# Splitting each tile's load over two DMA queues and moving the stores to GpSimd, in a GELU-and-multiply kernel

## The chip, the cores and the metric

The kernel runs on one core of one Trainium2 chip. The metric is the device time of one execution in microseconds; the kernel before takes 469.43 us, the median of 3 runs (469.3 to 469.44). A core has several engines with an instruction stream each. Here ScalarE (ACT in the profile) computes the GELU, VectorE (DVE) the product, and SyncE (SP), ACT and GpSimd (POOL) can issue DMA transfers. All transfers of the core, whoever issues them, are carried by 16 DMA engines; each issuing engine has a queue of its own to them.

## The reference

```python
def setup_inputs():
    batch, seq, dim = (32, 512, 2048)
    return {'x': np.random.randn(batch, seq, dim).astype(np.float32)}

def reference(x: np.ndarray) -> np.ndarray:
    half_dim = x.shape[-1] // 2
    x1, x2 = (x[..., :half_dim].copy(), x[..., half_dim:].copy())
    gelu_x1 = 0.5 * x1 * (1 + erf(x1 / np.sqrt(2)))
    return (gelu_x1 * x2).astype(np.float32)
```

The input has 16384 rows of 2048 float32 (134.2 MB), the output 16384 rows of 1024 (67.1 MB). Each output element is the GELU of an element of the left half of its row times the element at the same place in the right half.

## The kernel before

The rows are cut into 16 tiles of 1024 rows. In a tile each of the 128 partitions holds R = 8 consecutive rows (lines 26 to 28), so one partition's share of a tile is one contiguous run in memory: 64 KB of input, 32 KB of output. There are two input buffers (`x_bufs`) and two output buffers (`o_bufs`); tile i uses number i % 2 of each (lines 30 and 31).

The kernel is written with semaphores by hand. `counted` adds an increment to an instruction and keeps the running total in `n`; a wait on `n[...]` is thus a wait for everything issued so far that counts on that semaphore. A DMA adds 16 when it is complete, a compute instruction 1. `load` (line 48) is always issued on SP. `store` (line 53) takes the queue to issue on; it waits there until `mul_done` has reached its running total.

Ahead of the loop (lines 63 to 73) ACT issues a transfer of 4 KB into a scrap tile, the "opening"; SP issues the lower half (rows 0 to 3 of every partition) and the upper half (rows 4 to 7) of tile 0, with a semaphore each (`first`), and the whole of tile 1.

The loop at line 75 then goes over the tiles. A tile is computed in steps: rows 0 to 4 and 5 to 7 for an ordinary tile; rows 0-1, 2-3 and 4-7 for the first and the last. For each step ACT computes the GELU from the left half of `x_bufs[k]` into `o_bufs[k]` (line 87), and DVE multiplies it in place by the right half (line 95). Before the first step of a tile, ACT waits for `ready[k]` (line 85). Both the load of tile i and the store of tile i - 2 count on this one semaphore, so the wait covers the new input and the free output buffer.

After the steps the tile is stored: tiles 1 to 13 whole, on ACT's queue (line 112); tile 0 in two halves, also on ACT (line 107); tile 14 whole and tile 15 in two halves on SP (lines 105 and 110). When tile i is multiplied, SP issues the load of tile i + 2 into the same buffer (lines 113 to 115). A store on ACT waits for the multiply in ACT's instruction stream, and the GELU of the next tile stands behind it.

At the end ACT waits for the opening transfer, the semaphores are cleared, and SP waits until the last stores have landed (line 125).

Of the kernel before, what the change touches and what calls it, by code (L numbers as in the profile page):

```python
# [1 line left out]

# [4 lines left out]

GELU = mybir.ActivationFunctionType.Gelu


@with_exitstack
def kernel(
    ctx: ExitStack,
    tc: tile.TileContext,
    x: bass.AP,
    out: bass.AP,
):
    nc = tc.nc
    P = nc.NUM_PARTITIONS

    x_flat = x.flatten_outer_dims()
    out_flat = out.flatten_outer_dims()
    n_rows, dim = x_flat.shape
    half = dim // 2

    R = 8
    x_t = x_flat.rearrange("(n p r) d -> n p r d", p=P, r=R)
    o_t = out_flat.rearrange("(n p r) d -> n p r d", p=P, r=R)
    n_tiles = x_t.shape[0]
    x_bufs = [nc.alloc_sbuf_tensor(f"x{k}_tile", [P, R, dim], x.dtype) for k in range(2)]  # L30
    o_bufs = [nc.alloc_sbuf_tensor(f"o{k}_tile", [P, R, half], out.dtype) for k in range(2)]

    first = [nc.alloc_semaphore(f"first{j}") for j in range(2)]
    ready = [nc.alloc_semaphore(f"ready{k}") for k in range(2)]
    gelu_done = nc.alloc_semaphore("gelu_done")
    mul_done = nc.alloc_semaphore("mul_done")
    tail_stored = nc.alloc_semaphore("tail_stored")
    opened = nc.alloc_semaphore("opened")  # L40
    scrap = nc.alloc_sbuf_tensor("scrap_tile", [8, 128], x.dtype)
    n = {sem.name: 0 for sem in [*first, *ready, gelu_done, mul_done, tail_stored, opened]}

    def counted(ins, sem, by):
        ins.then_inc(sem, by)
        n[sem.name] += by

    def load(i, rows, sem):
        ins = nc.sync.dma_start(out=x_bufs[i % 2][:, rows, :], in_=x_t[i][:, rows, :])  # L49
        counted(ins, sem, 16)  # L50
        return ins

    def store(queue, i, rows, sem):
        queue.wait_ge(mul_done, n[mul_done.name])
        counted(
            queue.dma_start(out=o_t[i][:, rows, :], in_=o_bufs[i % 2][:, rows, :]), sem, 16
        )

    opening = nc.scalar.dma_start(out=scrap[:, :], in_=x_t[0][:8, 0, :128])
    counted(opening, opened, 16)
    for ins in (
        opening,
        load(0, slice(0, 4), first[0]),
        load(0, slice(4, 8), first[1]),
        load(1, slice(0, 8), ready[1]),
    ):  # L70
        tc.no_tile_sem_insts.add(ins.ins.name)
    tc.close()
    tc.compile()  # L73

    for i in range(n_tiles):
        k = i % 2
        last = i == n_tiles - 1
        pieces = i == 0 or last
        steps = ((0, 2), (2, 4), (4, 8)) if pieces else ((0, 5), (5, 8))
        for lo, hi in steps:  # L80
            rows = slice(lo, hi)
            if i == 0 and lo % 4 == 0:
                nc.scalar.wait_ge(first[lo // 4], 16)
            elif lo == 0:
                nc.scalar.wait_ge(ready[k], n[ready[k].name])
            counted(
                nc.scalar.activation(  # L87
                    out=o_bufs[k][:, rows, :], in_=x_bufs[k][:, rows, :half], func=GELU
                ),
                gelu_done,  # L90
                1,
            )
            nc.vector.wait_ge(gelu_done, n[gelu_done.name])
            counted(
                nc.vector.tensor_mul(  # L95
                    out=o_bufs[k][:, rows, :],
                    in0=o_bufs[k][:, rows, :],
                    in1=x_bufs[k][:, rows, half:],
                ),
                mul_done,  # L100
                1,
            )
            if pieces and hi % 4 == 0:
                if last:
                    store(nc.sync, i, slice(hi - 4, hi), tail_stored)
                else:
                    store(nc.scalar, i, slice(hi - 4, hi), ready[k])
        if not pieces:
            if i == n_tiles - 2:
                store(nc.sync, i, slice(0, R), tail_stored)  # L110
            else:
                store(nc.scalar, i, slice(0, R), ready[k])
        if i + 2 < n_tiles:
            nc.sync.wait_ge(mul_done, n[mul_done.name])
            load(i + 2, slice(0, R), ready[k])


    nc.scalar.wait_ge(opened, 16)
    nc.scalar.drain()  # L119
    for sem in (*first, *ready, opened):  # L120
        nc.scalar.sem_clear(sem)
    nc.vector.drain()
    nc.vector.sem_clear(gelu_done)
    nc.sync.sem_clear(mul_done)
    nc.sync.wait_ge(tail_stored, n[tail_stored.name]).then_inc(
        tail_stored, -n[tail_stored.name]
    )


# [1 line left out]
_INS = ['x']  # L131
_OUTS = [((32, 512, 1024), 'float32')]


# [23 lines left out]
```

## Time and profile before

| | |
|---|---|
| time, median of 3 runs | 469.43 us |
| profiled execution: span | 467.8 us (467.84 in the trace) |
| memory read and written | 134.22 MB and 67.11 MB, 430 GB/s over the span |
| ACT, GELU of 5 rows and 3 rows of a tile together | 7.12 us |
| DVE, product of the same | 8.76 us |
| load of a tile, from issue to landing, median | 44.4 us |
| store of a tile from ACT, from issue to landing, median | 44.7 us |
| first GELU starts | 12.79 us |
| last multiply starts | 455.76 us |

The span goes from the first to the last event of the program in one profiled execution; the time of a run has a little more around it. The profile names an engine, a line of the kernel and the operands of each group of instructions, and what ended the idle time before it. Issuing a transfer is not counted as work of its engine: such instructions appear as SPq or ACTq, with the duration of the issue alone. The records of the DMA queues count packets: a packet is one contiguous run of one partition, or a 4-byte write that adds to a semaphore. The DMA share is the mean busy share of the 16 engines; in a short stretch it can read above 1, since a packet is counted where it lands.

### The profile page before, as it was taken

The page shows a single profiled execution, that of the slowest core. Times are in us where ns is not written, and L with a number is a line of the kernel's source. Part 1 is how long each engine was busy: PE and PEld are TensorE (multiplying, and loading weights), DVE is VectorE, ACT ScalarE, POOL GpSimd, SP SyncE. Part 2 cuts the span into 40 slices and gives each one's busy share as a digit, 9 for nine tenths or more (in the row PEclk, how much of TensorE's full clock was granted, in tenths as well). Part 3 has the DMA queues.
Part 4 walks back from the last instruction along what each step waited for, and adds up shares of the span by engine and source line. Part 5 has one row for each costly group of instructions (what it writes and reads, how often), then busy time and mean ns, then how long its engine had stood idle before and what let it go on. Part 6 is the DMA issues. An engine that isn't in the chain of part 4 may idle for free.

```text
span 467.8 us, 154 instructions
## 1 busy us (share of the span) xinstructions
DVE 140.5 (30%) x34; ACT 115.5 (25%) x35; POOL 0.2 (0%) x4
## 2 busy tenths in 40 slices
DVE  0330515207051060511606115060150702507043
ACT  1320606041060410604105050050501506014060
POOL 0000000000000000000000000000000000000000
DMA  8999999999999999999999999999999999999988
GB/s 359 448 448 448 398 406 496 403 403 448 459 437 403 440 412 493 403 403 448 487 409 403 445 406 493 403 403 448 493 403 403 448 426 471 403 426 426 493 384 379
DMA packets 5057, 201.34 MB, mean 430 GB/s; under 512 B 568, under 2 KB 576, under 8 KB 576
## 3 DMA queue, kind: packets, MB, share of 16 engines
q1 hardware_dynamic: 2880, 142.61, 70.6%
q10 hardware_dynamic: 2176, 58.73, 29.1%
q14 instruction: 1, 0.01, 0.0%
HBM read 134.22 MB, written 67.11 MB: 430 GB/s over the span
## 4 chain that ended last, share of the span: by engine, by line
DMA 76%; DVE 14%; ACT 8%; ACTq 0%; SPq 0%; issue 0%
DMA out_dram<-o_tile 66%; DVE o_tile L95 14%; DMA x_tile<-in_x_dram 10%; ACT o_tile L87 8%; ACTq L119 0%; SPq L49 0%
## 5 line engine op out<-in xcount | busy, mean ns | idle before, releaser
L95 DVE TENSOR_TENSOR o_tile<-o_tile,x_tile 128x5120 f32<-128x5120 f32 (+3 forms) x34 | 140.5, 4171 | 319.7 <-ACT o_tile L87 319.7
L87 ACT ACTIVATE o_tile<-x_tile 128x5120 f32<-128x5120 f32 (+3 forms) x34 | 114.3, 3407 | 337.3 <-DMA out_dram<-o_tile 301.8
L87 ACT ACT_TABLE_LOAD x1 | 1.3, 1283 | 2.9 <-PEq L73 2.9
L142 POOL MEMSET const-bfloat16-1.0<- 128x1 bf16 x1 | 0.1, 102 | 0.0
L142 POOL MEMSET const-uint8-127<- 128x1 uint8 x1 | 0.1, 101 | 0.0
L142 POOL MEMSET const-float32-0.0<- 128x1 f32 x1 | 0.1, 99 | 0.2 <-issue 0.2
L142 POOL MEMSET const-float32-1.0<- 128x1 f32 x1 | 0.1, 98 | 0.0
## 6 DMA issues: line engine op xcount, KB each, us to landing
out_dram<-o_tile ACTq DMA_DIRECT2D x13, 4096.0 KB, 44.7
x_tile<-in_x_dram SPq DMA_DIRECT2D x2, 4096.0 KB, 16.7
out_dram<-o_tile ACTq DMA_DIRECT2D x2, 2048.0 KB, 34.4
out_dram<-o_tile SPq DMA_DIRECT2D x1, 4096.0 KB, 25.2
out_dram<-o_tile SPq DMA_DIRECT2D x2, 2048.0 KB, 7.8
x_tile<-in_x_dram SPq DMA_DIRECT2D x15, 44.4
scrap_tile<-in_x_dram ACTq DMA_DIRECT2D x1, 4.0 KB
```

The costliest lines, as they stand in the source:

```text
L87: nc.scalar.activation(out=o_bufs[k][:, rows, :], in_=x_bufs[k][:, rows, :half], func=GELU),
L95: nc.vector.tensor_mul(out=o_bufs[k][:, rows, :], in0=o_bufs[k][:, rows, :], in1=x_bufs[k][:, rows, half:],),
L142: nc = _bacc.Bacc("TRN2", target_bir_lowering=False, num_devices=1)
```

## The change

A tile's load becomes two transfers: rows 0 to 3 of each partition on SP's queue and rows 4 to 7 on ACT's, 32 KB per partition each. Tile 0 still comes wholly on SP. Tile 1's upper half is issued by ACT once tile 0's lower half has landed. For later tiles ACT waits for the multiply of tile i and then issues the upper half of tile i + 2. The stores of tiles 0 to 13 are issued by GpSimd, which has nothing else to do; the last two tiles are stored from SP as before. Since loads and stores are now on different queues, the stores get semaphores of their own (`stored`), and ACT waits for `ready[k]` and then `stored[k]` before a tile. The opening transfer and its wait at the end are gone. The computation, its steps and the two buffers of each kind stay.

```diff
-    opened = nc.alloc_semaphore("opened")
-    scrap = nc.alloc_sbuf_tensor("scrap_tile", [8, 128], x.dtype)
-    n = {sem.name: 0 for sem in [*first, *ready, gelu_done, mul_done, tail_stored, opened]}
+    stored = [nc.alloc_semaphore(f"stored{k}") for k in range(2)]
+    n = {sem.name: 0 for sem in [*first, *ready, *stored, gelu_done, mul_done, tail_stored]}
...
-    def load(i, rows, sem):
-        ins = nc.sync.dma_start(out=x_bufs[i % 2][:, rows, :], in_=x_t[i][:, rows, :])
+    def load(queue, i, rows, sem):
+        ins = queue.dma_start(out=x_bufs[i % 2][:, rows, :], in_=x_t[i][:, rows, :])
...
-    opening = nc.scalar.dma_start(out=scrap[:, :], in_=x_t[0][:8, 0, :128])
-    counted(opening, opened, 16)
+    lower, upper = slice(0, 4), slice(4, 8)
     for ins in (
-        opening,
-        load(0, slice(0, 4), first[0]),
-        load(0, slice(4, 8), first[1]),
-        load(1, slice(0, 8), ready[1]),
+        load(nc.sync, 0, lower, first[0]),
+        load(nc.sync, 0, upper, first[1]),
+        load(nc.sync, 1, lower, ready[1]),
     ):
...
             if i == 0 and lo % 4 == 0:
                 nc.scalar.wait_ge(first[lo // 4], 16)
+                if lo == 0:
+                    load(nc.scalar, 1, upper, ready[1])
             elif lo == 0:
                 nc.scalar.wait_ge(ready[k], n[ready[k].name])
+                if n[stored[k].name]:
+                    nc.scalar.wait_ge(stored[k], n[stored[k].name])
...
-                    store(nc.scalar, i, slice(hi - 4, hi), ready[k])
+                    store(nc.gpsimd, i, slice(hi - 4, hi), stored[k])
...
-                store(nc.scalar, i, slice(0, R), ready[k])
+                store(nc.gpsimd, i, slice(0, R), stored[k])
         if i + 2 < n_tiles:
             nc.sync.wait_ge(mul_done, n[mul_done.name])
-            load(i + 2, slice(0, R), ready[k])
+            load(nc.sync, i + 2, lower, ready[k])
+            nc.scalar.wait_ge(mul_done, n[mul_done.name])
+            load(nc.scalar, i + 2, upper, ready[k])
...
-    nc.scalar.wait_ge(opened, 16)
     nc.scalar.drain()
-    for sem in (*first, *ready, opened):
+    for sem in (*first, *ready, *stored):
         nc.scalar.sem_clear(sem)
```

## The prediction

> **What bounds the kernel now.** I read the page's share of each DMA queue first, then a stretch of the steady state by queue, then the same stretch by engine, and last the chain of waits around the first and the last tiles.
>
> ```profile
> span 467.8 us, 154 instructions
> DVE 140.5 (30%) x34; ACT 115.5 (25%) x35; POOL 0.2 (0%) x4
> q1 hardware_dynamic: 2880, 142.61, 70.6%
> q10 hardware_dynamic: 2176, 58.73, 29.1%
> ```
>
> q1 is SP's queue, q10 ACT's: 70.6% + 29.1% = 99.7% of the time of all 16 DMA engines lies inside packets, while the two compute engines stand idle for 70% and more. The DMA queues from 118 to 350 us, eight tiles in 232 us, and then the engines of one tile pair:
>
> ```profile
> DMA packets 2304, 100.66 MB, mean 434 GB/s; under 512 B 256, under 2 KB 256, under 8 KB 256
> q1 hardware_dynamic: 1152, 67.11, 66.7%
> q10 hardware_dynamic: 1152, 33.55, 33.5%
> ```
> ```profile
> 118.00:176.00 58.00, 17.52 (x4) 14.24 (x4) 0.00 (x0) 1.00 1.00 434
> ```
>
> Here the DMA share is 1.00. Of the 1152 packets on each queue 128 are the 4-byte semaphore writes; the other 1024 are one row group of one partition each, 64 KB for a load and 32 KB for a store. A load packet takes 0.667 x 232 x 16 / 1024 = 2.418 us, a store packet 0.335 x 232 x 16 / 1024 = 1.214 us. The sum of 100.2% says that neighbouring packets overlap a little. The packet records of the trace give it exactly: durations 2418 and 1213 ns, but from start to start on one engine 2414 and 1209 ns, and this whether the next packet is from the same queue or the other. So a byte costs the same for loads and stores, a switch between two queues costs nothing, and no engine pauses from 2.2 us (first load packet) to 467.4-467.8 us (last semaphore writes). Tile 1 in the timeline, and tile 3 in the chain of waits (start, duration, what):
>
> ```profile
> 47.02 7.12 ACT L87 ACTIVATE o_tile<-x_tile 128x5120 f32<-128x5120 f32 x2 [20.93 <-DMA x_tile<-in_x_dram]
> 51.52 8.76 DVE L95 TENSOR_TENSOR o_tile<-o_tile,x_tile 128x5120 f32<-128x5120 f32 x2 [20.97 <-ACT o_tile L87]
> ```
> ```profile
> 100.40 4.48 ACT o_tile L87
> 104.88 0.02 issue
> 104.91 8.77 DVE o_tile L95 x2
> 113.68 0.02 issue
> 113.70 44.67 DMA out_dram<-o_tile
> ```
>
> A tile that has landed is computed in 113.68 - 100.40 = 13.3 us and then spends 44.7 us in the queues. One tile's store and the next load to the same buffer, 12.58 MB, keep the engines busy for 29.0 us (58.0 us a pair, 434 GB/s). At 100.38 us they still hold a whole such batch for the other buffer, and the next is issued 13.3 us later. **The time is the sum of the packets; the waits in the chain are waits for a queue that never runs dry.** A change matters if it alters that sum, lets the queues run dry, or alters the two ends.
>
> **The change, part by part.** *Split loads.* Tiles 1 to 15 were loaded in 64-KB packets, 8 per engine and tile (128 partitions over 16 engines): 120 packets per engine become 240 of 32 KB. From start to start 2 x 1209.3 - 2414.1 = 4.5 ns more for each of the 120: +0.54 us. If durations count without the overlap, 2 x 1213 - 2418 = 8 ns: +0.96. I take 0.54, since start to start is what a full engine repeats.
>
> *Semaphore writes.* Loads go from 17 to 32 issues, each with one 4-byte packet of 9 ns on every engine: 15 x 9 = 0.135 us, less the opening transfer's one: +0.13.
>
> *The opening transfer* (8 packets of 512 B at 25 ns, on ACT's queue at 2.15 us) goes. The first load packets start at 2.20 us and take 1.64 to 2.06 us, mean 1.81, instead of 1.21. If that came from the opening transfer beside them, 0.6 us would be won; if it is the start of the reads themselves, nothing. A 25-ns packet can hardly cost 600: I take 0, bounds -0.6 and 0.
>
> *Issues.* SP's load issues (0.33 us each) stay 17: two halves of tile 0, one half each of the 15 others. ACT's 15 store issues (0.36) become 15 load issues; GpSimd gets 15 stores. ACT waits for the same multiply before its load as it did before its store, and what is queued behind it, the next tile's GELU, needs its tile landed anyhow: in the chain ACT waits there for 21.9 us. The new wait for the store of two tiles ago was inside the old wait (one semaphore counted both). On SP nothing stands behind a load but the next one and the last three stores; on POOL (busy 0.2 us) nothing stands behind a store but the next, 29 us later. All issue time lies under queues with a backlog.
>
> *GpSimd's issue latency.* No row has a store from GpSimd. From SP the way from issue to first packet is 2.20 - 0.73 = 1.5 us. A steady store is issued behind the previous tile's traffic, which lasts 29.0 - 13.3 = 15.7 us more; a longer way costs nothing until it reaches about 13 us. I take 0.
>
> *GpSimd's packets.* Not shown either. From below: if the eight rows that an engine has of a store go as one packet, 7 seams of 4.5 ns vanish in each of 15 stores: -0.5 us. From above: if every store's first packet on every engine started cold like the first packets of the run (+0.43 to +0.85 us), 15 stores give +6 to +13 us. The nearest row is ACT's store packets, the same rows between the same loads, 1209 ns from start to start: I take 0 and keep -0.5 and +13.
>
> *Order at the start.* Tile 0's upper half now shares with the upper half of tile 1, issued on ACT at 12.8 us when tile 0's lower half has landed, and from about 21 us with the first store. Worked through by turns of 32 KB: tile 0's upper half lands near 33 us (22.4 before), its multiply ends near 41 (30.6), tile 1's lower half lands near 51.5 (47.0), its upper half well ahead. Work issued by then ends at 2.8 + 38.7 (16.78 MB) + 29.0 = 70.5 us, so 19 us are queued, against 13.3 + 1.5 = 14.8 needed until the next batch moves. Nothing runs dry; about 4 us of cover are left, where before it was far more. The lead of the upper halves (some 11 us) then stays, and later tiles keep about 7 us.
>
> *The end.* When tile 15 lands (448.5 us), the store of tile 14 (4.19 MB, 9.7 us) is left. It stands behind tile 15's lower half in SP's queue, as before behind the whole tile. The first half of tile 15's store moves 455.1 - 448.5 + 1.5 = 8.1 us later, the second 460.2 - 448.5 + 1.5 = 13.2 against 9.7 + 4.8 = 14.5: covered by 1.3 us, and the last store lands as now.
>
> Sum: 0.54 + 0.13 = +0.67 us. The profiled execution: 467.84 + 0.67 = 468.5 span. The median of the runs lies 469.43 - 467.84 = 1.6 us above that span, so **470.1 us**, +0.14%. About 0.2% (0.94 us) is what a measurement can tell from no change; by that this is none.
>
> **The rivals.** *(B) GpSimd's packets are dearer: slower.* Place: the 120 store packets per engine on the third queue. Every nanosecond there adds 0.12 us; it decides from 2.3 ns, where 0.67 + 0.27 passes 0.94. For it: no GpSimd store is in the trace, and with DMA share 1.00 nothing can hide even a small cost on one engine, as tiles wait for all 16. Against: two queues alternate without any cost now. A cold start of 0.43 us per store gives 470.1 + 6.5 = 476.6; 20 ns a packet, 472.5. The Trainium skill (DMA: Bandwidth & Descriptors, "Latency and other measured facts") holds engines 7 and 15 to be usually slower with software-generated descriptors, which is how GpSimd issues, and gives no size; in this trace, which has none, all 16 engines end within 0.45 us of each other.
>
> *(C) The stores starve and the queues run dry: much slower.* If the engines take turns by packet and GpSimd's packets are far smaller than 32 KB (say 4 KB), two load queues take nearly all turns. Both buffers then fill with landed tiles, and only the older store, 9.7 us, is left while the next tile is computed and its batch started: 14.8 us. That leaves some 5.1 us idle per pair of tiles, 7 pairs: +36 us, about 507 with the extra seams (7 x 4.5 ns x 112 = 3.5 us). For it: taking turns by packet is seen, since a 64-KB load and a 32-KB store issued together land within 0.3 us (44.4 and 44.7 us). Against: every queue's packets here are as long as the contiguous run. The Trainium skill (same page, "SWDGE vs HWDGE vs iDMA") states 4096 B as the preferred packet; this trace's packets of 64 KB on the hardware queues disagree, and no run shows GpSimd's.
>
> *(D) Not slower.* The slow first packets were the opening transfer's doing and go with it: 470.1 - 0.6 = 469.5; with seams saved on the stores, 469.0. Both are still no change. For faster by 0.2% (468.5) no row offers enough: the engines are full from 2.2 us to the end.
>
> **How the numbers follow.** Forecast 0.46, own range 469.7 to 470.7 (the 8-ns seam reaches 470.5); B 0.36, mostly below 476; C 0.07; D 0.11. Range 469.0 to 476.0: it leaves out C and the far end of B, some 0.13, and a little of D. Faster 0.05 (from D). Same: 0.37 of the forecast and 0.06 of D, 0.43. Slower: 0.09 of the forecast (dearer seams), B and C, 0.52. The single likeliest case is no change, though all slower cases together weigh more.
>
> **What would show it.** Right: DMA share 1.00 and 433 to 434 GB/s in the steady stretch, three queues near 33% each, 32-KB packets of 1213 ns on all, the pair period up by 0.07 us. The store's time to landing may fall and the load halves differ by some 11 us without meaning. B shows as more time per packet on GpSimd's queue, or as one or two engines ending late; C as stretches of DMA share below 1.00 and small packets; D as first packets near 1.2 us. The forecast is wrong if DMA share drops below 1.00 anywhere between 3 and 467 us.

## The result and the profile after

| | before | changed |
|---|---|---|
| time, median of 8 runs | 469.29 us (469.19 to 469.53) | 470.52 us (470.45 to 470.73) |
| ratio | | 1.0027 (95% interval 1.0018 to 1.0035) |
| span of the profiled execution | 467.84 us | 469.2 us (469.16 in the trace) |

The changed kernel is 1.23 us slower. That is a small but real loss: the runs of the two kernels do not overlap. The first lines and the DMA queues of the changed kernel's page (packets, MB, share of 16 engines over the span):

```profile
span 469.2 us, 183 instructions
...
q1 hardware_dynamic: 2880, 79.69, 39.6%
q10 hardware_dynamic: 2160, 62.92, 31.1%
q0 software_dynamic: 2160, 58.72, 29.0%
```

q0 is GpSimd's queue. The three shares add up to 99.7%, exactly as the two did before: the engines are as full as they were, and the span is longer because they have more to do. The same queues in the steady window from 118 to 350 us, and the chain of waits (start, duration, what):

```profile
q0 software_dynamic: 1152, 33.55, 33.5%
q1 hardware_dynamic: 1152, 33.55, 33.5%
q10 hardware_dynamic: 1151, 33.52, 33.5%
```
```profile
116.92 44.77 DMA x_tile<-in_x_dram
...
175.00 44.77 DMA x_tile<-in_x_dram
...
233.09 44.76 DMA x_tile<-in_x_dram
...
349.27 44.76 DMA x_tile<-in_x_dram
```

All three queues carry 1024 packets of 32 KB (one fewer on q10 in this window) and 128 semaphore writes in the same time: 0.335 x 232 x 16 / 1024 = 1.214 us a packet, GpSimd's like the others. In the packet records, packets on one engine mostly follow each other from start to start in 1209 ns, whichever two queues they come from.

A seam is what two 32-KB packets take more than one of 64 KB. Four pairs of tiles take 349.27 - 116.92 = 232.35 us, where they took 345.70 - 113.70 = 232.00; the chain of before has:

```profile
113.70 44.67 DMA out_dram<-o_tile
...
345.70 44.73 DMA out_dram<-o_tile
```

That is 0.09 us more for a pair (0.0875), as 16 seams of 4.5 ns and 2 semaphore writes of 9 ns make it. The 15 split tiles are 7.5 pairs: 0.66 us over the run.

The rest is lost once, around the first store. The queues from 20 to 32 us, before and then changed:

```profile
q1 hardware_dynamic: 96, 4.72, 93.3%
q10 hardware_dynamic: 48, 0.79, 15.3%
```
```profile
q10 hardware_dynamic: 69, 2.26, 45.0%
q1 hardware_dynamic: 73, 1.87, 42.7%
q0 software_dynamic: 43, 0.70, 13.7%
```

From this view one can work out by how much packets are stretched, that is, how much longer they take than in the steady state. The view counts a packet, with its whole duration, in the window in which it starts. 100% is 12 us x 16 engines = 192 us. From a queue's share of that goes what its packets take in the steady state, and the remainder over 16 is the loss per engine. Before, q1 has 64 packets of 64 KB, 16 of 32 KB and 16 semaphore writes: 179.1 - 174.3 = 4.8, so 0.30 us per engine. Changed, q1 has 57 of 32 KB (1.87 MB): 82.0 - 69.3 = 12.7, 0.79 us; q10 has 69: 86.4 - 83.7 = 2.7, 0.17 us; q0's are on time. Together 0.96 us, 0.66 more than before. With the 0.66 above that is 1.32, and the spans differ by 469.16 - 467.84 = 1.32.

### The profile page after: what moved, and what is told of

Same layout as the page of the kernel before. It is cut to its first block, busy times and chain, and to the rows that moved or that the text cites. A ratio compares the mean times of both kernels' runs of the same rounds, so it can differ in the third digit from the quotient of the medians.

```text
span 469.2 us, 183 instructions
## 1 busy us (share of the span) xinstructions
DVE 140.5 (30%) x34; ACT 115.5 (25%) x35; POOL 8.3 (2%) x19
## 4 chain that ended last, share of the span: by engine, by line
DMA 76%; DVE 14%; ACT 8%; ACTq 0%; issue 0%
DMA x_tile<-in_x_dram 76%; DVE o_tile L92 14%; ACT o_tile L84 8%; ACTq L117 0%
## 5 line engine op out<-in xcount | busy, mean ns | idle before, releaser
L55 POOL DMA_DIRECT2D out_dram<-o_tile x15 | 8.1, 542 | 399.6 <-DVE o_tile L92 399.6
```

## The experiments

All times are against the kernel before, run beside them on the same chip (469.25 to 469.28 us). "Stretch" is the loss per engine computed as above. In the code cuts "..." marks lines left out.

**Stores on GpSimd alone** (the kernel before, loads whole on SP).

```diff
...
-                    store(nc.scalar, i, slice(hi - 4, hi), ready[k])
+                    store(nc.gpsimd, i, slice(hi - 4, hi), stored[k])
...
-                store(nc.scalar, i, slice(0, R), ready[k])
+                store(nc.gpsimd, i, slice(0, R), stored[k])
...
```

> The kernel before, with only the stores of tiles 0 to 13 moved to GpSimd and their own semaphores; loads whole on SP in 64-KB packets. Theory 'GpSimd's queue is only dear when it starts': steady packets 1213 ns as on ACT, but load packets stretched by 0.6 to 1.0 us per engine around the first store: +0.3 to +0.7 us against before. Rival 'seams and the second load queue do it all': +0.0 us. Rival 'GpSimd's packets are dearer': more than 1213 ns per store packet in the steady stretch; 20 ns would give +2.4 us.

469.25 us, ratio 0.9999 (0.999 to 1.0007). From 20 to 32 us:

```profile
q1 hardware_dynamic: 96, 4.72, 92.6%
q0 software_dynamic: 48, 0.79, 15.3%
```

The same packets as before in a little less time: 0.22 us of stretch. The "dear when it starts" theory falls; moving the stores to GpSimd's queue costs nothing that these runs can measure, at its start or later.

**No opening transfer** (the kernel before without it).

```diff
-    opening = nc.scalar.dma_start(out=scrap[:, :], in_=x_t[0][:8, 0, :128])
-    counted(opening, opened, 16)
...
```

> The kernel before without the opening transfer on ACT. Theory 'a queue's first use costs a stretch of the packets around it': the stretch at 20 to 32 us grows from 0.3 towards 1.0 us per engine, +0.3 to +0.7 us. Rival 'the opening does nothing': the same time as before within 0.1%, and the first load packets are as slow as with it (mean 1.8 us).

469.35 us, 1.0002 (0.9993 to 1.001). The opening does nothing that can be measured: the first 16 load packets take 1.83 us in the mean without it, 1.81 with it.

**Split loads alone, both halves on SP.**

```diff
-        load(1, slice(0, 8), ready[1]),
+        load(1, slice(0, 4), ready[1]),
+        load(1, slice(4, 8), ready[1]),
...
-            load(i + 2, slice(0, R), ready[k])
+            load(i + 2, slice(0, 4), ready[k])
+            load(i + 2, slice(4, 8), ready[k])
```

> The kernel before, with the loads of tiles 1 to 15 in two halves of 32-KB packets, both on SP; stores stay on ACT. Theory 'seams': 120 packets per engine become 240, 4.5 ns each, and 15 more semaphore writes of 9 ns: +0.54 to +0.58 and +0.13, so +0.7 us against before (about 470.0), and the load packets around the first store (20 to 32 us) stay as little stretched as before (0.3 us per engine). Rival 'it is the 32-KB packets as such': the stretch around the first store, 1.0 us per engine in the changed kernel, appears here too and the run is +1.2 us slower. Unequal turns (32 KB for a load, 32 KB for a store) let the store finish sooner; no engine should run dry.

471.21 us (470.72 to 475.1), 1.0058 (1.0037 to 1.008): more than either number. The stretch around the first store is there although one queue does all loading (0.86 us per engine). Loads and stores now alternate 32 KB to 32 KB, so a store is done in 25.5 us and ACT's queue stands empty for a while in each tile. By the packet records, packets are stretched again later, by 0.58 us per engine in sum between 118 and 445 us: load packets soon after a store is issued on the empty queue (1342 and 1380 ns at 243 us on two engines, for 1213), and packets of some stores themselves (up to 1629 ns at 167 us). Seams 0.66, 0.86 - 0.30 around the first store and this 0.58 are 1.80; the span is 1.79 longer. What starts the later ones is not shown.

**Tile 1 alone in halves** (the other tiles whole, all on SP).

```diff
-        load(1, slice(0, 8), ready[1]),
+        load(1, slice(0, 4), ready[1]),
+        load(1, slice(4, 8), ready[1]),
```

> The kernel before, with one edit: tile 1 alone is loaded in two halves of 32-KB packets, both on SP. Eight seams and one semaphore write per engine are worth 0.05 us. Theory 'small load packets around the first store are stretched more': the load packets from 20 to 32 us lose about 0.8 us per engine instead of 0.3, so +0.5 us against before. Rival 'the stretch there comes from the second load queue': 0.3 us as before and +0.05 us in all.

469.66 us, 1.0013 (1.0004 to 1.0022), +0.41 us. From 20 to 32 us:

```profile
q1 hardware_dynamic: 127, 3.64, 76.8%
q10 hardware_dynamic: 78, 1.28, 24.8%
```

111 packets of 32 KB: 147.5 - 134.8 = 12.7, 0.79 us per engine, with neither GpSimd nor a second load queue. Smaller load packets around the first store are enough for it.

**The first store moved.** Is it the store that stretches them, or SP's step from tile 0 to tile 1 at the same time? Here tile 0 is stored whole after its last multiply, issued at 30.65 instead of from 19.25 us; tile 1 is in halves as in the last run.

```diff
-            if pieces and hi % 4 == 0:
+            if pieces and (hi % 4 == 0 if last else hi == 8):
...
-                    store(nc.scalar, i, slice(hi - 4, hi), ready[k])
+                    store(nc.scalar, i, slice(0, R), ready[k])
```

> The kernel before with tile 1 loaded in two 32-KB halves on SP, as in an earlier run, and in addition tile 0 stored whole after its last multiply (30.6 us) instead of in two halves from 19.3 us. Theory 'the first store of the run stretches the load packets around it': the stretched load packets move from 19-25 us to about 32-38 us, and the stretch from 20 to 30 us falls to nearly nothing. Rival 'SP's step from tile 0 to tile 1 stretches them': they stay at 20 to 25 us.

469.87 us (one run). From 20 to 30 us, and from 30 to 42:

```profile
q1 hardware_dynamic: 144, 4.19, 97.1%
```
```profile
q1 hardware_dynamic: 112, 3.15, 68.8%
q10 hardware_dynamic: 48, 1.57, 30.3%
```

At first 128 packets in 155.4 us, 1.21 us each: nothing is stretched while SP steps from tile to tile. Then 96 packets in 132.1 us less 16 semaphore writes, 1.37 us each: 0.97 us per engine. The stretch went where the store went. By the packet records the stretched packets start at 32.6 to 34.8 us: after the store is issued, and before its own first packet at 35.97. So the slowing begins before the store's data moves.

The same edit in the changed kernel (first store issued at 36.94 us):

> The changed kernel, with tile 0 stored whole after its last multiply (about 39 us) instead of its first half at 21.3 us. Theory 'the first store stretches the packets around it': the stretch at 23 to 28 us goes and a like one appears from about 40 us; time +1.0 to +1.5 us against before. Rival 'two load queues side by side stretch each other': the stretch stays at 23 to 28 us. With 2 MB less queued when tile 1 lands, some of the cover of 4 us goes; if the queues run dry there it is up to +4 us.

470.66 us, 1.0031 (1.0018 to 1.0044). From 20 to 30 us, with two load queues side by side, and from 30 to 42:

```profile
q10 hardware_dynamic: 69, 2.26, 52.3%
q1 hardware_dynamic: 75, 1.93, 44.8%
```
```profile
q1 hardware_dynamic: 111, 3.64, 74.0%
q10 hardware_dynamic: 64, 1.57, 34.2%
q0 software_dynamic: 1, 0.03, 0.6%
```

First 69 packets in 83.7 us: 1.213 each, so two load queues do not stretch each other. Then 0.46 us on each load queue: it follows the store here too, and the queues did not run dry.

**Tile 1 whole in the changed kernel**, ACT's queue starting with tile 2.

```diff
-        load(nc.sync, 1, lower, ready[1]),
+        load(nc.sync, 1, slice(0, 8), ready[1]),
...
-                if lo == 0:
-                    load(nc.scalar, 1, upper, ready[1])
```

> The changed kernel, with tile 1 loaded whole (64-KB packets) on SP at the start, so that ACT's queue starts with tile 2's upper half. Theory 'small load packets around the first store': the stretch at 20 to 32 us falls from 1.0 to 0.3 us per engine; tile 2's upper half then passes tile 1, which by turns of one 64-KB packet to one of 32 KB should land near 53 us and leave the queues just covered: about +0.5 us against before. If tile 1 lands after 56 us the queues run dry and it is +1 to +6 us. Rival 'halves that run in step are stretched all through': this depends on how far apart the two halves land; under 3 us apart, +6 us and more; some 7 us apart, nothing.

470.63 us, 1.0034 (1.0022 to 1.0046). The stretch from 20 to 32 us fell as expected (92.4% for the same 96 packets, 0.19 us), but ACT's packets lose 0.5 us between 53 and 60 us, so nothing was won. What starts there was not found; the first store had long begun.

**Tile 1's upper half on SP from the start.** Only the place of one issue differs from the changed kernel.

```diff
         load(nc.sync, 1, lower, ready[1]),
+        load(nc.sync, 1, upper, ready[1]),
...
-                if lo == 0:
-                    load(nc.scalar, 1, upper, ready[1])
```

> The changed kernel, with the upper half of tile 1 issued on SP at the start instead of on ACT at 12.8 us, so that ACT's queue starts only with tile 2. Theory 'a third queue starting beside two busy ones stretches the packets': with one load queue busy at the first store, the stretch at 20 to 32 us falls from 1.0 to about 0.3 us per engine, and the run is 0.6 us faster than the changed kernel (about +0.6 us against before), unless ACT's queue makes the same stretch when it starts at about 31 us. Rival 'GpSimd's first issue does it': stretch stays near 1.0 us and the time at +1.2 us. The tile halves should land within a few us of each other.

485.29 us, 1.0346 (1.0332 to 1.0359): 16 us slower, which no theory had. The stretch from 20 to 32 us did not fall to 0.3 but to 0.56 us. Its chain of waits, and its engines around 70 us (window, length, busy time of DVE, ACT and POOL, clock, DMA share, GB/s):

```profile
30.75 0.38 ACTq L48
31.13 30.38 another core or an unknown queue
61.51 0.02 issue
61.53 4.48 ACT o_tile L83
```
```profile
60.00:68.00 8.00, 1.97 (x1) 6.47 (x2) 0.00 (x0) 1.00 1.06 459
68.00:78.00 10.00, 6.79 (x2) 3.36 (x2) 0.53 (x1) 1.00 0.55 203
```

ACT issues tile 2's upper half at 30.75 us onto its empty queue, where it passes tile 1, still waiting on SP: it lands at 58.7 us, tile 1's upper half at 61.1. While tile 1 is computed, only tile 2's lower half is left, and the engines stand still for almost half of the 10 us from 68. The changed kernel avoids this by issuing tile 1's upper half on ACT early: this is the cover of which the prediction saw about 4 us left.

The dry spell explains some 5 us, and another, shorter one comes at the end (DMA share 0.49 from 468 to 472 us). Between them the engines are busy and yet slower: from 118 to 350 us the shares add up to 100.3%, but 425 GB/s are moved where the changed kernel moves 434.

```profile
DMA packets 3396, 98.70 MB, mean 425 GB/s; under 512 B 384, under 2 KB 384, under 8 KB 384
q10 hardware_dynamic: 1130, 32.83, 33.8%
q1 hardware_dynamic: 1131, 32.87, 33.6%
q0 software_dynamic: 1135, 33.00, 32.9%
```

The load packets are stretched here, to 1241 ns in the mean on SP's queue and 1251 on ACT's, by the packet records, while GpSimd's store packets take 1213. By the shares that is 2.4 and 1.8 us per engine, about 1 us per pair of tiles. Beside it stands another sign, in the semaphore writes, one per engine, that end each transfer: the time from the first of the 16 to the last, by the packet records, for the loads of tiles 3, 7, 11 and 15 on SP.

```
                              tile 3   tile 7   tile 11   tile 15 (us)
before                          0.3      0.3      0.3       0.4
changed                         0.5      0.5      0.5       0.5
tile 1's upper half on SP       0.6      3.2      4.0       4.8
all halves issued at once       0.6      2.1      3.6       5.2
```

In this run both halves of a tile land together (105.6 us for tile 3 on both queues), and the engines drift apart. A tile waits for the slowest. The changed kernel's upper halves land 3.6 us ahead of the lower ones (99.6 and 103.2 us), and its engines stay together. The next run has nearly the same drift with hardly a stretched packet from 118 to 350 us, so the two are not one thing; why the packets are stretched here is not shown.

**All halves issued at once**, tile 0's and 1's too, so that nothing passes.

```diff
-        load(nc.sync, 0, upper, first[1]),
+        load(nc.scalar, 0, upper, first[1]),
         load(nc.sync, 1, lower, ready[1]),
+        load(nc.scalar, 1, upper, ready[1]),
...
-                if lo == 0:
-                    load(nc.scalar, 1, upper, ready[1])
```

> The changed kernel, with every tile split between SP and ACT from the start, tiles 0 and 1 too, all four halves issued at once. No tile passes another, so nothing should run dry. Theory 'two halves of one tile read in step stretch the packets' (as the run with tile 1's upper half on SP showed after its dry stretch, 1.2 us per pair of tiles): +6 to +9 us against before, with both halves landing within 1 us and packets above 1213 ns in the steady stretch. Rival 'only running dry cost time there': +0.7 to +1.5 us, like the changed kernel.

473.04 us (471.67 to 475.78), 1.0083 (1.0057 to 1.0109): between the two. Nothing runs dry early, the steady shares are 33.5% as in the changed kernel, but the engines drift (last row above) and the loss comes at the end. Around the first store, issued at 29.48 us, these 32-KB load packets lose only 0.28 us per engine (28 to 40 us), and ACT's another 0.57 at 42 us, where no cause was found. The last tile's GELUs in the timeline, and the engines in that window:

```profile
454.42 7.22 ACT L83 ACTIVATE o_tile<-x_tile 128x2048 f32<-128x2048 f32 x3 [21.06 <-DMA out_dram<-o_tile]
```
```profile
454.00:462.00 8.00, 4.83 (x3) 7.22 (x3) 0.00 (x0) 1.00 0.59 252
```

The last tile waits for the store of tile 13, the last thing to land. DMA share falls to 0.59 for 8 us. The reading is that the engines that are ahead have by then moved most of tile 14's store, the only cover of the end.

**Loads in quarters** (16-KB packets, all on SP; four `load` calls of two rows each in place of one).

> The kernel before with the loads of tiles 1 to 15 in four transfers of 16-KB packets, all on SP. Theory 'seams': 4 x 607 - 2414 = 14 ns for each of 120 packets, +1.7 us, and 45 more semaphore writes of 9 ns, +0.4 us: +2.1 us, and up to 0.7 us more around the first store, +2.8 us at most. Rival 'seams cost nothing': within 0.3 us of before plus the stretch. A 16-KB packet should read 611 ns in the steady stretch.

477.12 us, 1.0167 (1.0151 to 1.0182): +7.9, far over the bound. A seam is priced right (607 ns from start to start), but the engines drift here too (8 us and more between the first and the last of a landing after 330 us), although one queue does all loading, and a part of them runs dry at the end. Seams alone do not price small packets.

**Stores row by row** (the changed kernel, 4-KB packets on GpSimd).

```diff
-                store(nc.gpsimd, i, slice(0, R), stored[k])
+                for r in range(R):
+                    store(nc.gpsimd, i, slice(r, r + 1), stored[k])
```

> The changed kernel, with the stores of tiles 1 to 13 issued on GpSimd row by row: 8 transfers of 4-KB packets per tile instead of one of 32-KB packets. Theory 'the engines take turns by packet': two load queues get nearly all turns, both input buffers fill, and 5 us per pair of tiles run dry; with 7 seams of 4.5 ns in each of 104 store packets per engine and 91 more semaphore writes about 505 to 515 us, DMA share below 1 at some point of each pair. Rival 'turns are by bytes': about 474 us (470.5 plus seams).

523.78 us, 1.116 (1.1141 to 1.118). In each pair of tiles the engines have a time like this one:

```profile
260.00:264.00 4.00, 4.00 (x2) 0.00 (x0) 0.00 (x0) 1.00 0.29 119
264.00:268.00 4.00, 1.31 (x1) 2.19 (x1) 2.36 (x5) 1.00 0.46 131
```

The engines idle for some 5 us (0.71 x 4 + 0.54 x 4) while the first of two landed tiles is computed. Turns by packet, by which a queue with small packets starves, give this; turns by bytes would not. The Trainium skill (DMA: Bandwidth & Descriptors, "Queues, rings and completion order") states that an engine changes queues at packet boundaries; this run agrees with it. The total is 9 us above the upper end expected, and load packets are stretched here too: from 118 to 350 us alone they lose 5 us per engine, by the packet records.

No run here beat the kernel before. Its engines are full from the first packet to the last; what its trace still shows to win is small: the slow first load packets (1.81 us for 1.21), the 0.30 us around the first store and the seams.

## Why the prediction was right or wrong

The measured time lies in the range and 0.4 us from the forecast, but the forecast called it no change, and it is slower: +1.23 us where 0.67 was worked out. The 0.2% that the prediction took as the least that can be told from no change lies inside the interval of the ratio (0.18 to 0.35%). Half of the sum was right and half was missing. That 470.52 still lies below the forecast's own upper end of 470.7 is luck, since that end stood for seams of 8 ns, which did not occur; and of the 0.52 given to slower, 0.43 stood for rivals B and C, which did not occur either.

- *What bounds the kernel:* right. The time is the sum of the packets, and the engines stay full. The shares, 99.7% of the span before and after and 33.5% per queue in the steady window, are what the prediction asked for. Its sign of being wrong, a DMA share below 1.00 anywhere from 3 to 467 us, could not serve: from 4 to 12 us the view gives 0.92 for both kernels.
- *Seams and semaphore writes:* right, 0.67 predicted and 0.66 measured. Start to start was the right price; 8 ns per seam would have given 1.09.
- *GpSimd's packets and latency, rival B:* taken as 0, and none shows: 1209 ns from start to start, and moving the stores alone gives 0.9999. The Trainium skill's slower engines 7 and 15 (same page, "Latency and other measured facts") do not show: in the changed kernel all 16 engines end a steady transfer within 0.5 us.
- *The opening transfer:* taken as 0, and it is; rival D falls with it, since the first packets of the run are as slow without it.
- *The mis-sized term:* "from start to start 1209.3" was used for every load packet. Around the first store it does not hold. In the trace of before this is visible (0.30 us per engine in the view from 20 to 32 us), and the prediction left it in the sum unchanged, as if it were a fixed cost of the run. With 32-KB packets there it is 0.96. That the first store sets its place is shown by the two runs that moved it. That halving the load packets there is enough to raise it is shown by tile 1 alone in halves (0.79 for 0.30) and, the other way, by tile 1 whole in the changed kernel (0.19 for 0.96). The size is not all of it: two runs with 32-KB packets lost 0.56 and 0.28 there. Why an engine loses time there is not shown.
- *The order at the start:* right that nothing runs dry. Tile 0's second GELU starts at 30.7 us and tile 1's first at 53.7, where about 33 and 51.5 were expected for the landings. The lead of the upper halves was 12.6 us at tile 1 (about 11 expected) and 7.5 at tile 2, but 3.6 from tile 3 on, where about 7 was to stay. Whether it is "without meaning" is open: in two runs in which it is nought the engines drift apart, in the run with stores row by row it is nought too and they do not. The prediction had no term for drift.
- *The end:* right for this kernel, which keeps its cover; the run with all halves at once shows what its loss costs.
- *Rival C:* right as a mechanism and not the case here: GpSimd's packets are 32 KB. With 4-KB packets it is what happens. Its own terms add up to 470.1 + 36 + 3.5 = 509.6, not 507.
- *A reading error:* the first load packet starts at 1.74 us and the last semaphore write ends at 467.4, not 2.2 and 467.8. The packet records had been set against the span 0.46 us too late. No term of the sum depends on it; the way from issue to first packet is 1.0 us, not 1.5.

## What to carry to other kernels

Where the DMA engines are full, price a change by its packets, from start to start, and look at the points where a queue begins, where packets can take longer than in the steady state. Moving large stores from ACT to GpSimd cost nothing measurable here. Splitting transfers over queues gives up the order between them: work out which transfer now passes which, how much is still queued when the next tile lands, and whether that covers a tile's computation. A tile waits for its slowest engine, so look at how far apart the 16 completions of one transfer lie; a mean of 434 GB/s does not show it.

## What was not expected of the hardware

- Load packets around the first store of a run are stretched, by 0.2 to 0.3 us per engine with 64-KB packets (four runs) and mostly by 0.8 to 1.0 with 32-KB ones; two runs with 32-KB packets had 0.56 and 0.28.
- The 16 engines can drift apart. With both halves of a tile landing at the same time from two queues the spread of a landing grew by about 0.4 us a tile, up to 5 us, in two runs; with the halves 3.6 us apart it stayed at 0.5, and in the run with tile 1 whole, 6.4 us apart, at 1.7 to 2.5. But halves in step are neither needed for it nor enough: with all loads on one queue the spread grew to 2 us (halves) and 8 us (quarters), and with stores row by row the halves land together and it stays at 0.4 to 0.9 from tile 3 on. The cause is open.
- A transfer on an empty queue beside busy ones is slow to begin: ACT's first load in the changed kernel is issued at 12.85 us and its first packet starts at 16.8, 4 us later; for the first load of the run that is 1.0 us.
